# Memory's keys first, its values behind the feed-forward, queries in two pairs: a planned kernel of two transformer blocks

## The chip, the cores and the metric

The kernel runs on one core of a Trainium2 chip. The metric is the device time of one execution in microseconds (us); the median of several runs counts. What is studied here is one change to this kernel and what it does to that time.

## What is computed

Two transformer blocks, one behind the other, on 256 tokens of width 1024, batch 1, all in fp32. The first block has a modulation from a condition vector `c`, a mixer of two halves and a gated feed-forward; the second has a pooling and a top-k attention mixer, a cross-attention to 256 memory tokens, and a mixture of 32 experts (two of them per token). Cut to the part that the change touches and its neighbours:

```python
def first_block(x, c, ...):
    cond = silu(c) @ ada_w + ada_b                 # six vectors of 1024
    h = modulate(rmsnorm(x), shift1, scale1)
    x = x + gate1 * (mixer(h @ w_in) @ w_out)
    h2 = modulate(rmsnorm(x), shift2, scale2)
    g_ff, up_ff = split(h2 @ w_ffn_in)
    x = x + gate2 * ((silu(g_ff) * up_ff) @ w_ffn_out)
    return modulate(rmsnorm(x), shift_f, scale_f)  # from c, too

def memory_cross_attention(h, mem, ...):           # 4 heads of 128
    m = rmsnorm_2(mem, g_mem)
    q = rmsnorm_2(h @ w_q, q_norm)
    k = rmsnorm_2((m @ w_kv)[first half], k_norm)
    v = (m @ w_kv)[second half]
    p = softmax(q @ k.T / sqrt(128))
    return (p @ v) @ w_o

def second_block(x, mem, ...):
    x = x + concat(pool_mixer(...), dsa_attention(...)) @ w_out
    x = x + memory_cross_attention(rmsnorm_2(x), mem, ...)
    return x + hierarchical_moe(rmsnorm_2(x), ...)  # router, 32 experts
```

The memory's keys and values depend on `mem` alone, on nothing that the first block computes.

## The kernel before

**A program that is planned.** The code does not issue instructions directly. Each call on an engine (`V` VectorE, `S` ScalarE, `G` GpSimd, `PE` TensorE, `SY` SyncE, whose queue issues the DMAs) is noted by a `Recorder` (from L425) with what it reads and writes. `flush` (L709) then gives all operations of a section an order, issues them, and so decides what stands behind what on each engine; `issue` holds the one line, L763, that the profile shows for all of them. `plan` (L571) is a list scheduler: it keeps a clock for each engine, takes among the ready operations of an engine the one that can begin first and, among those that could begin now, the one of the highest priority. Priorities come from a pass backwards through the order found (`back`); `flush` repeats this in 30 rounds with random noise on the priorities and keeps the shortest plan. An operation that is ready early can thus be drawn far ahead of its place in the code, into a time in which its engine would wait.

**Memory.** 24 regions `R` (`NREG`, L246) of 128 x 2048 fp32 (1 MB) take the activations and, one after the other, the weights. These come as one long `stream` in the order of `plan()` (L211): memory's keys `mk` and values `mv` head that list, `ada` is the modulation's weights, `in_gv`, `in_v`, `in_u`, `out` are the first mixer, `fin` and `fout` the feed-forward, `in2...` and `out2` the second mixer, `wq` and `wo` the cross-attention, `gu` and `dn` the experts (96 regions). A region that is given back is filled by the next load in SP's order. 8 banks `B` of PSUM take the products.

**Products.** A weight that is used as fp32 is loaded in pieces of 1024 columns; `piece` splits each into a rounded part (ScalarE copies it to fp32r) and the rest (VectorE subtracts), and a product is then three products of 256 columns (`mm`). The halves live in smaller pools cut from regions (`rec.host`): P0, P1, P2, P3 for stages of the program (`splits`, with the numbers of `SPLITS`), and M for memory's `mk` and `mv` alone. `dense4` makes four 128-row outputs with 96 products; `moving` makes token-major outputs with 48 products of 512 columns. In the profile such operands are all called R. An fp32 product (not fp32r) leaves two records in the trace.

**The places that the change touches.** `memory()` (L1547 to 1575) makes memory's keys `km` and values `vm`: it splits `mt` (the memory, token columns), sums its squares, multiplies by `mk` (`dense4`), normalizes the keys (`k_norm_mem`), and multiplies by `mv` (`moving`). It is called at L1664, behind the second mixer's `in2v`. `mt` is loaded by a call at L1535, where `ahead` also names `mk`. Cross-attention stands at L1680 to 1742: norm `rx_` by `norm_col`, queries `wq` (`dense4`), their norm `rmq`, then for four units (head pair i, token half t) scores, maximum, exponential (`lm`), the reciprocal, transposes (`pm`), and the product with `vm`; then `wo`. `warm` (L1170, called at L1374) issues four fp32 products of `ones` by a sum, ahead of the feed-forward's norm. `xt` (x, token columns) is the first load behind the constants (L842).

Of the kernel before, what the change touches and what calls it, by code (L numbers as in the profile page):

```python
# [11 lines left out]
ALU = mybir.AluOpType  # L12
# [82 lines left out]
def layout(v):  # L95
# [51 lines left out]
    for name, arg in PLAN:  # L147
# [37 lines left out]
        elif name == "wq":  # L185
            full(rowk(wq))
# [30 lines left out]
def plan():  # L217
# [12 lines left out]
    p += [("out2", 0), ("out2", 1), ("wq", 0), ("wo", 0)]  # L230
# [10 lines left out]
def size(name, arg):  # L241
    return {("in2", 3): 1024, ("fout", 5): 2048, ("misc", 0): 3072}.get(
        (name, arg), 4096)


NREG = 24  # L246
SPLITS = (5, 6, 5, 2)
# [176 lines left out]

class Recorder:  # L425
# [3 lines left out]
    def __init__(self, nc, pools):  # L429
# [4 lines left out]
        self.total = 0.0  # L434
# [118 lines left out]
    def plan(self, prio):  # L553
# [49 lines left out]
        while len(order) < n:  # L603
# [33 lines left out]
            c = op.cost  # L637
            if op.eng == "vector" and now["gpsimd"] > t:
                c += min(c, now["gpsimd"] - t)
# [16 lines left out]
            done[op.pos] = True  # L656
            order.append((op, t, t + c))
# [53 lines left out]
    def flush(self):  # L711
# [8 lines left out]
        best, rng = None, np.random.default_rng(SEED)  # L720
        for i in range(ROUNDS):
            p = self.plan(prio)
            if best is None or p[0] < best[0]:
                best = p
                rank = [0.0] * len(ops)
                for op, s, e in p[1]:
                    rank[op.pos] = e
                base = -np.array(self.back(rank, p[4]))
                prio = list(base)
            else:  # L730
                prio = list(base + NOISE * rng.standard_normal(len(ops)))
        self.total, order, place, self.slots, _ = best
        for op, op.start, op.end in order:
# [7 lines left out]
        self.ops, self.chain = [], None  # L741

# [26 lines left out]
ROUNDS = 30  # L769
SEED = 2  # L770
NOISE = 0.5
# [9 lines left out]
def _build(tc, a, out, ctx):  # L781
# [7 lines left out]
    def region(i):  # L789
# [4 lines left out]
                        "s": tiles(20, "s", 16), "B": tiles(8, "B", 512, psum)})  # L794
# [47 lines left out]
    SY.dma_start(out=xt, in_=a["xt"])  # L842
    stage = [None]
# [20 lines left out]
    G.memset(ones, 1.0)  # L864
    inv_d = fixed(1, "inv_d")
# [26 lines left out]
    def piece(name):  # L892
# [5 lines left out]
        b = buf("M" if name in ("mk", "mv") else stage[0], 2, 1024, dt=F32R)  # L898
# [37 lines left out]
    def dense4(name, act_, pieces=range(4), ps=None):  # L936
# [4 lines left out]
        for i in pieces:  # L941
            w = piece(name)
            for kk in range(2):
                k = 2 * i + kk
                for n in range(4):
                    c = slice(512 * kk + 128 * n, 512 * kk + 128 * n + 128)
                    mm(ps[n], at(w, slice(None), c), at(act_, slice(None), k),
                       k == 0 and n % 2 == 0, k == KT - 1)
        return ps
# [88 lines left out]
    def norm_col(accs, inv):  # L1038
# [6 lines left out]
        r = small(2)  # L1045
# [124 lines left out]
    def warm(after, n):  # L1170

        ps = bank()[:, 0:T]
        for i in range(n):
            PE.matmul(out=ps, lhsT=ones, rhs=after, start=True, stop=True)

# [9 lines left out]

    sums = Sums()
# [187 lines left out]
    warm(sq2.acc[0], 4)  # L1374
# [34 lines left out]

# [137 lines left out]
    def memory():  # L1547
        for i in range(3):
            rec.host("M", Reg(), 2048)
# [447 lines left out]
```

## Time and profile before

| | |
|---|---|
| median of 3 runs | 761.04 us (759.38 to 765.29) |
| profiled execution | 763.06 us, its span 761.2 us |
| TensorE busy | 711.6 us, 93% |
| VectorE, ScalarE busy | 416.7 us (55%), 312.6 us (41%) |
| loaded | 210.48 MB, 278 GB/s over the span |

How to read it: the page divides the span into 40 slices of 19 us and gives the busy tenths of each engine in each. The chain that ended last is followed back from the last instruction, at each step to what released it. The windows give for a stretch of the span each engine's busy time with its number of records (PE, PEld, DVE, ACT, POOL in this order), then the granted TensorE clock as a share of 2.4 GHz, the DMA engines' mean share and GB/s. PE is TensorE's products, PEld its weight loads, DVE VectorE, ACT ScalarE, SP the engine that issues the loads. Because all operations are issued from one line, L763, the operands' names and shapes tell which is which: `inv_d`, `inv_h`, `ones` are constants, `cst` the table with the identity, `xt`, `mt` and `stream` the arrays in HBM. A busy PE is not a PE at its peak: the ends of products are modelled from the records around them.

### The profile page before, as it was taken

To read this page: it belongs to the slowest core of one execution; us is meant where nothing else is said; L and a number is where in the kernel's file an instruction comes from. 1 tells how busy PE (TensorE), PEld (TensorE's weight loads), DVE (VectorE), ACT (ScalarE), POOL (GpSimd) and SP (SyncE) were. 2 spreads that over 40 slices of the span, in tenths; PEclk is the share of its full clock that TensorE was granted. 3 is DMA by queue.
4 is the path that set the end of the run, shared out by engine and by line. 5 is a ranking of instruction groups with operands and counts; after the bars stand their busy time and mean duration, and the time that the engine had idled before them with its cause. 6 is when DMAs were issued, how large, how long until landed. Compare 5 with 4: busy or idle time off the path is not lost.

```text
span 761.2 us, 13000 instructions
## 1 busy us (share of the span) xinstructions
PE 711.6 (93%) x5290; PEld 555.6 (73%) x5290; DVE 416.7 (55%) x872; ACT 312.6 (41%) x597; POOL 6.9 (1%) x18
## 2 busy tenths in 40 slices
PE   4799999999999999999999999999899999987794
PEld 1487756889999999999999779898854455432231
DVE  3579847786556583797868988465612121100002
ACT  3366467233544352386845439365512111110010
POOL 0020000000000000000000000000000000000000
PEclk9999998979999999999999999999899999998898
DMA  8993689988465765743114214798879999999993
GB/s 362 420 418 139 246 311 412 370 338 314 167 215 188 262 228 174 277 139 126 65 65 127 95 56 176 237 384 303 350 292 420 422 419 421 421 421 420 421 415 127
DMA packets 31168, 212.42 MB, mean 279 GB/s; under 512 B 3584, under 2 KB 3968, under 8 KB 6272
## 3 DMA queue, kind: packets, MB, share of 16 engines
q1 hardware_dynamic: 31104, 211.55, 71.1%
q8 instruction: 43, 0.70, 0.4%
q14 instruction: 21, 0.17, 0.1%
HBM read 210.48 MB, written 1.05 MB: 278 GB/s over the span
## 4 chain that ended last, share of the span: by engine, by line
PE 76%; DMA 16%; DVE 5%; ACT 1%; issue 1%; SPq 0%; ACTq 0%; DVEq 0%
PE B L763 76%; DMA R<-stream 15%; DVE R L763 4%; DMA R<-xt 1%; DVE s L763 1%; DVE U L763 1%; ACT R L763 0%; ACT L763 0%; SPq L763 0%; ACT U L763 0%; ACT ex L763 0%; DVE cond L763 0%; DVE g L763 0%; DVE ng L763 0%; ACT s L763 0%
## 5 line engine op out<-in xcount | busy, mean ns | idle before, releaser
L763 PE MATMUL B<-R,R 128*128 128x256 f32 (+4 forms) x4376 | 592.7, 376 | 27.9 <-DVE R L763 12.8
L763 PEld LDWEIGHTS B<-R,R 128*128 128x128 f32 (+2 forms) x4376 | 436.5, 171 | 114.6 <-issue 48.7
L763 ACT ACTIVATE R<-R 128x1024 fp32r<-128x1024 f32 (+3 forms) x268 | 187.0, 737 | 168.0 <-PE B L763 120.1
L763 DVE TENSOR_TENSOR R<-R,R 128x1024 fp32r<-128x1024 f32 (+3 forms) x214 | 191.5, 930 | 62.6 <-ACT R L763 55.5
L763 DVE TENSOR_TENSOR R<-B,R 128x256 f32<-128x256 f32 (+3 forms) x78 | 33.0, 440 | 89.2 <-ACT R L763 57.2
L763 ACT ACTIVATE R<-B 128x256 f32<-128x256 f32 (+4 forms) x82 | 27.9, 370 | 80.3 <-PE B L763 80.2
L763 ACT ACTIVATE R<-B,cv 128x128 f32<-128x128 f32 (+2 forms) x64 | 25.9, 423 | 80.5 <-PE B L763 79.9
L763 PEld LDWEIGHTS B<-U,R 128*128 128x128 f32 x256 | 34.9, 196 | 28.7 <-issue 22.1
L763 PE MATMUL B<-R 128*128 128x256 f32 (+4 forms) x200 | 48.9, 378 | 1.2 <-ACT R L763 1.2
L763 DVE TENSOR_SCALAR R<-B,cv 128x128 f32<-128x128 f32 x32 | 11.1, 350 | 67.3 <-PE B L763 65.2
L763 PEld LDWEIGHTS B<-R 128*128 128x128 f32 (+1 forms) x200 | 30.9, 192 | 17.9 <-issue 12.6
L763 PE MATMUL B<-U,R 128*128 128x128 f32 x256 | 41.9, 294 | 1.8 <-DVE s L763 1.0
L763 ACT COPY R<-B 128x256 f32<-128x256 f32 (+3 forms) x35 | 13.7, 408 | 69.6 <-PE B L763 69.4
L763 DVE COPY R<-B 128x256 f32<-128x256 f32 (+2 forms) x33 | 14.8, 462 | 38.6 <-PE B L763 38.4
L763 DVE SCALAR_TENSOR_TENSOR U<-R,ca,U 128x512 f32<-128x512 f32 x42 | 31.4, 749 | 0.7
L763 DVE SCALAR_TENSOR_TENSOR R<-R,cv,R 128x256 f32<-128x256 f32 (+1 forms) x54 | 25.0, 481 | 1.8 <-ACT R L763 1.2
L763 ACT ACT_TABLE_LOAD x17 | 21.8, 1283 | 9.9 <-PE B L763 6.3
L763 PE MATMUL B<-cst,R 128*128 128x128 f32 (+3 forms) x130 | 21.8, 271 | 3.2 <-DVE R L763 3.2
L763 PEld LDWEIGHTS B<-cst,R 128*128 128x128 f32 (+1 forms) x130 | 17.6, 170 | 8.6 <-DVE R L763 5.7
L763 DVE TENSOR_TENSOR R<-R 128x256 f32<-128x256 f32 x47 | 18.2, 420 | 2.4 <-ACT R L763 1.8
L763 PE MATMUL B<-R,cst 128*128 128x256 f32 (+1 forms) x52 | 16.0, 400 | 0.1
L763 ACT ACTIVATE R<-R,cv 128x256 fp32r<-128x256 f32 (+1 forms) x28 | 12.8, 496 | 2.2 <-DVE R L763 2.1
(116 smaller groups left out, 266.0 us busy)
## 6 DMA issues: line engine op xcount, KB each, us to landing
R<-stream SPq DMA_DIRECT2D x192, 1024.0 KB, 10.4
R<-stream SPq DMA_DIRECT2D x10, 512.0 KB, 15.3
R<-xt SPq DMA_DIRECT2D x1, 1024.0 KB, 5.3
R<-mt SPq DMA_DIRECT2D x1, 1024.0 KB, 7.8
out_dram<-R SPq DMA_DIRECT2D x4, 256.0 KB, 2.1
cst<-cst SPq DMA_DIRECT2D x1, 533.0 KB, 19.6
R<-bands SPq DMA_DIRECT2D x1, 320.0 KB, 3.2
R<-cosin SPq DMA_DIRECT2D x1, 256.0 KB, 5.4
```

Of the source, the lines that this page charges most:

```text
L763: getattr(getattr(self.nc, op.eng), name)(*[real(v) for v in args], **{k: real(v) for k, v in kw.items()})
```

## The change

1. `memory()` stands at the start of the program, ahead of everything but the constants, without the values; `mt` (in two halves) and `mk` are loaded ahead of `xt`. `mk`'s and `mv`'s pieces take the stage's pool, and pool M is gone.
2. The values are a function of their own, `memory_values()`, called behind the feed-forward's last accumulation, ahead of the first block's final norm.
3. `wq` is loaded as two halves of 2048 columns, and cross-attention runs over two pairs of heads: `dense2` (48 products), norm, scores, softmax, product with `vm`, one pair behind the other.
4. 26 regions instead of 24 (`dynamic_dma_scratch_size=1024` at the build gives room); SPLITS (5, 6, 3, 2) instead of (5, 6, 5, 2), pool P3 made at the feed-forward's end already, with 2 of 5 pieces of stage P2 going to it; 18 small tiles instead of 20.
5. `warm` is gone. Where the planner sees TensorE wait longer than FILL_MIN, it puts `filler` products (`ones` by `ones`, 128 columns) into a free bank ahead of the waiting product.
6. Priorities: instead of 30 rounds with noise and the shortest plan, a list of 19 steps (`PATH`), each a pass backwards plus a `nudge`: seeded shifts of whole stretches of the program, by engine.

```diff
-            full(rowk(wq))
+            full(rowk(wq[:, 256 * arg:256 * arg + 256]))
...
-NREG = 24
-SPLITS = (5, 6, 5, 2)
+NREG = 26
+SPLITS = (5, 6, 3, 2)
...
+            if op.eng == "tensor":
+                k = min((f, i) for i, f in enumerate(slots["B"] + [1e9]) if f is not None)
+                lo = max(now["tensor"], k[0])
+                room = t - lo
+                m = int(max(FILL * room, room - FILL_END) / FILLER) if room > FILL_MIN else 0
...
-        best, rng = None, np.random.default_rng(SEED)
-        for i in range(ROUNDS):
-            p = self.plan(prio)
...
+        best = self.plan(prio)
+        for seed in PATH if self.first else (0,):
...
+            best = self.plan(list(nudge(at, seed) - np.array(self.back(rank, best[4]))))
...
+    def filler(self, m, k):
+        ones = self.ones.ap()
+        for i in range(m):
+            self.nc.tensor.matmul(out=self.pools["B"][k][:, 0:128], lhsT=ones, rhs=ones, start=True,
+                                  stop=True)
...
+FILLER, FILL, FILL_MIN, FILL_END = 0.224, 0.4, 0.7, 1.2
+PATH = (0, 4, 0, 31, 36, 0, 63, 0, 88, 120, 121, 144, 195, 343, 433, 447, 465, 779, 910)
...
-    SY.dma_start(out=xt, in_=a["xt"])
...
-        b = buf("M" if name in ("mk", "mv") else stage[0], 2, 1024, dt=F32R)
+        pool = stage[0]
+        if pool == "P2":
+            turn[0] += 1
+            pool = "P3" if turn[0] % 5 in (2, 4) else "P2"
+        b = buf(pool, 2, 1024, dt=F32R)
...
+    for k in (0, 4):
+        SY.dma_start(out=mt[:, k:k + 4], in_=a["mt"][:, k:k + 4])
+        if k == 0:
+            ahead("mk", 0, 2)
+    SY.dma_start(out=xt, in_=a["xt"])
+    rmem_ = fixed(2, "rmem", constant=False)
+    mem = memory()
...
-    warm(sq2.acc[0], 4)
...
+    splits("P3", SPLITS[3])
     splits("P2", SPLITS[2])
+    memory_values()
...
-    memory()
     attended(sums)
...
-    splits("P3", SPLITS[3])
+    stage[0] = "P3"
...
-    ps = dense4("wq", h)
...
+    for i in range(2):
+        ps = dense2("wq", h)
+        pr = bank()
```

What the planner makes of it is seen in the order of the instructions. The first place is the head of SP's queue, the loads in the order in which they are issued; the names are a region with its buffer's number, and the array in HBM. Before:

```order
L763 DMA cv<-cv 128x296
L763 DMA cst<-cst 128x164
L763 DMA R_0_144<-xt 128x2048
L763 DMA R_0_147<-stream 128x2048
L763 DMA R_0_155<-stream 128x2048
L763 DMA R_0_170<-stream 128x2048
L763 DMA R_0_180<-stream 128x2048
```

and of the change:

```order
L797 DMA cv<-cv 128x296
L797 DMA cst<-cst 128x164
L797 DMA R_0_143<-mt 128x1024
L797 DMA R_0_145<-stream 128x1024 x2
L797 DMA R_0_152<-stream 128x1024 x2
L797 DMA R_0_143<-mt 128x1024
L797 DMA R_0_219<-xt 128x2048
L797 DMA R_0_235<-stream 128x2048
L797 DMA R_0_264<-stream 128x2048
```

Ahead of `xt` there now stand `mt` in two halves and four loads of half a region each, the two regions of `mk`; the first `ada` region (`R_0_235`) follows `xt`.

The second place is TensorE at the end of the feed-forward. Before, where `R_7_3168` and `R_7_3213` are the split memory, rounded part and rest, and `R_2_3299` and `R_6_3300` regions with pieces of `mk`:

```order
L763 MATMUL B_89<-R_7_3213,R_6_3300 128x256
L763 MATMUL B_89<-R_7_3168,R_6_3300 128x256
L763 MATMUL B_87<-R_7_3168,R_2_3299 128x256
L763 MATMUL B_87<-R_7_3213,R_2_3299 128x256
L763 MATMUL B_88<-inv_d,R_0_157 128x1 x4
L763 MATMUL B_87<-R_7_3168,R_2_3299 128x256 x2
L763 MATMUL B_87<-R_7_3213,R_2_3299 128x256
L763 MATMUL B_87<-R_7_3168,R_2_3299 128x256
L763 MATMUL B_87<-R_7_3168,R_6_3300 128x256
L763 MATMUL B_87<-R_7_3213,R_6_3300 128x256
```

and of the change, where the first row is the last of the feed-forward's accumulation `R_0_154` and `R_0_158` are the split memory and `R_2_3632` holds a piece of `mv`:

```order
L797 MATMUL B_84<-R_4_1991,R_4_1360 128x256 x6
L797 MATMUL B_82<-ones,U_62 128x1 x4
L797 MATMUL B_87<-R_2_3632,R_0_154 128x512
L797 MATMUL B_83<-R_2_3632,R_0_154 128x512
L774 MATMUL B_85<-ones 128x128
L797 MATMUL B_87<-R_2_3632,R_0_154 128x512
L797 MATMUL B_87<-R_2_3632,R_0_158 128x512
L797 MATMUL B_85<-inv_d,R_0_216 128x1 x4
L797 MATMUL B_87<-R_2_3632,R_0_154 128x512
L797 MATMUL B_83<-R_2_3632,R_0_154 128x512
```

The one-column sums of the final norm (`inv_d`) now stand between 512-column products of `mv`, where before they stood between 256-column products of `mk`; a filler (`ones` by nothing else, L774) is among them.

The third place is TensorE in cross-attention, behind the products of `wq`. Before, with transposes (`cst`) of the softmax, and the products of `mv` as the 512-column rows:

```order
L763 MATMUL B_89<-R_2_3299,R_7_3168 128x512 x2
L763 MATMUL B_90<-R_6_3300,R_7_3168 128x512
L763 MATMUL B_90<-R_6_3300,R_7_3213 128x512
L763 MATMUL B_86<-cst,R_9_4984 128x128 x2
L763 MATMUL B_89<-R_2_3299,R_7_3213 128x512
L763 MATMUL B_89<-R_6_3300,R_7_3168 128x512
L763 MATMUL B_90<-R_6_3300,R_7_3168 128x512 x2
L763 MATMUL B_84<-cst,R_9_4984 128x128 x2
L763 MATMUL B_89<-R_6_3300,R_7_3168 128x512
L763 MATMUL B_90<-R_6_3300,R_7_3213 128x512
L763 MATMUL B_89<-R_6_3300,R_7_3213 128x512
```

and of the change, with the last product of `wq` at the top (`inv_h` makes the column sums of the queries' norm, and the rows with `R_0_400`, which is `km`, are the scores):

```order
L797 MATMUL B_81<-R_3_4884,R_2_3515 128x256
L797 MATMUL B_86<-inv_h,R_0_216 128x1 x4
L797 MATMUL B_87<-R_0_400,R_4_3911 128x256 x2
L797 MATMUL B_85<-inv_h,R_0_216 128x1 x4
L797 MATMUL B_88<-R_0_400,R_4_3911 128x256 x2
L797 MATMUL B_82<-R_0_400,R_4_3911 128x256 x2
L797 MATMUL B_83<-R_0_400,R_4_3911 128x256 x2
L774 MATMUL B_86<-ones 128x128 x5
L797 MATMUL B_84<-cst,R_6_5061 128x128 x2
L797 MATMUL B_86<-cst,R_6_5061 128x128 x2
```

Between the scores and the transposes there now stand five fillers, and no product of `mv` or `wq`: the last `wq` product of the second pair is ahead of the first pair's sums.

## Rows read from the trace of the kernel before

**Rows 1.** The page: the chain that ended last, shares of the span by engine.

```profile
PE 76%; DMA 16%; DVE 5%; ACT 1%; issue 1%; SPq 0%; ACTq 0%; DVEq 0%
```

**Rows 2.** The page: busy tenths in 40 slices, TensorE and DMA.

```profile
PE   4799999999999999999999999999899999987794
...
DMA  8993689988465765743114214798879999999993
```

**Rows 3.** The chain in order of time: start us, us, what.

```profile
27.50 13.32 PE B L763 x82
...
40.85 0.18 DVE cond L763
...
43.82 101.40 PE B L763 x840
...
157.49 250.86 PE B L763 x2052
...
430.16 117.32 PE B L763 x805
...
726.60 16.29 DMA R<-stream
```

**Rows 4.** Timeline of SP's issues up to 562 us: start us, us, operation, count.

```profile
485.75 58.88 SPq L763 DMA_DIRECT2D R<-stream  x21
...
555.93 5.76 SPq L763 DMA_DIRECT2D R<-stream  x5
```

**Rows 5.** Windows: stretch, its us, busy of five engines, clock, DMA share, GB/s.

```profile
43.40:46.80 3.40, 2.98 (x14) 2.98 (x15) 3.40 (x7) 0.91 (x1) 3.40 (x1) 0.51 1.02 424
...
152.60:162.80 10.20, 8.96 (x40) 8.19 (x39) 8.77 (x24) 3.01 (x7) 0.00 (x0) 0.50 1.02 430
...
385.00:410.00 25.00, 25.00 (x193) 22.01 (x192) 16.13 (x41) 12.00 (x30) 0.00 (x0) 1.00 0.18 53
410.00:430.00 20.00, 20.00 (x133) 18.03 (x131) 20.00 (x68) 13.28 (x24) 0.00 (x0) 1.00 0.29 102
430.00:440.00 10.00, 9.95 (x34) 6.17 (x34) 9.37 (x23) 2.09 (x3) 0.00 (x0) 0.83 0.32 104
495.50:540.50 45.00, 45.00 (x319) 42.22 (x318) 27.43 (x63) 25.68 (x60) 0.00 (x0) 1.00 0.90 351
540.50:556.00 15.50, 13.39 (x87) 11.51 (x89) 9.45 (x52) 8.15 (x17) 0.00 (x0) 0.67 0.60 237
...
557.00:743.00 186.00, 167.79 (x1158) 74.87 (x1158) 26.90 (x67) 23.99 (x59) 0.00 (x0) 0.97 1.01 418
```

**Rows 6.** Timeline of TensorE: start us, us, operation, count [idle before, releaser].

```profile
9.62 1.94 PE L763 MATMUL B<-R,R 128*32 128x512 f32 x8 [9.62 <-DVE R L763]
...
109.26 1.07 PE L763 MATMUL B<-R,R 128*32 128x512 f32 x8
...
326.81 25.44 PE L763 MATMUL B<-R,R 128*128 128x256 f32 x210
...
357.96 0.95 PE L763 MATMUL B<-inv_d,R 128*128 128x1 f32 x8
...
514.44 6.82 PE L763 MATMUL B<-R,R 128*128 128x512 f32 x29
...
548.58 0.64 PE L763 MATMUL B<-asum,cst 128*128 128x32 f32 x2 [1.11 <-DVE asum L763]
...
551.92 2.48 PE L763 MATMUL B<-U,R 128*128 128x128 f32 x10 [1.00 <-DVE s L763]
...
556.65 1.38 PE L763 MATMUL B<-U,R 128*128 128x128 f32 x10
...
559.82 0.49 PE L763 MATMUL B<-U,R 128*128 128x128 f32 x2
```

**Rows 7.** Timeline of ScalarE in the softmax of the cross-attention.

```profile
516.77 1.28 ACT L763 ACT_TABLE_LOAD   x1 [2.57 <-DVE s L763]
518.07 0.56 ACT L763 ACTIVATE R<-B,s,s 128x256 f32<-128x256 f32 x1
```

More of the change, by code (lines that the diff above doesn't have):

```diff
@@ L602, in plan @@
                 offer(op)
-        while len(order) < n:
+        issued = 0
+        while issued < n:
             best = None
@@ L948, in dense4, with dense2 @@
                        k == 0 and n % 2 == 0, k == KT - 1)
+        return ps
+    def dense2(name, act_):
+        b = bank()
+        ps = [b[:, T * i:T * i + T] for i in range(2)]
+        for i in range(2):
+            w = piece(name)
+            for kk in range(4):
+                k = 4 * i + kk
+                for n in range(2):
+                    c = slice(256 * kk + 128 * n, 256 * kk + 128 * n + 128)
+                    mm(ps[n], at(w, slice(None), c), at(act_, slice(None), k),
+                       k == 0 and n == 0, k == KT - 1)
         return ps
@@ L1184, in stacked, with memory, k_norm_mem, memory_values @@
         return w.rearrange("p (b m) c -> p b m c", b=4)
+    def memory():
+        hm = pair()
+        for k in range(KT):
+            split(hm, k, mt[:, k], scale=col("mn", k))
+        sums = Sums()
+        for k in range(KT):
+            sums.add(mt[:, k])
+        rmem = norm_col(sums.acc, inv_d, rmem_)
+        rmem2 = square(rmem)
+        def k_norm_mem(j, ps):
+            q = ta()
+            S.activation(out=q, in_=ps, func=AF.Square)
+            S.activation(out=km[:, j], in_=ps, func=AF.Copy, scale=col("xk_norm"))
+            p2 = bank()
+            for t in range(2):
+                PE.matmul(out=p2[:, t:t + 1], lhsT=q[:, 128 * t:128 * t + 128], rhs=inv_h, start=True,
+                          stop=True)
+            rk = small(2, 1)
+            rstd_by(rk, p2[:, 0:2].unsqueeze(2), rmem, rmem2)
+            V.tensor_tensor(out=km[:, j], in0=km[:, j], in1=norm_bc(rk[:, :, 0]), op=ALU.mult)
+        for j, ps in enumerate(dense4("mk", hm)):
+            k_norm_mem(j, ps)
+        return hm, rmem
+    def memory_values():
+        hm, rmem = mem
+        ps = moving("mv", hm)
+        for t in range(2):
+            S.activation(out=vm[:, t], in_=ps[t], func=AF.Copy, scale=rmem[:, t:t + 1])
+    for k in (0, 4):
[5 more added lines that the diff above has]
+    mem = memory()
     sums = Sums()
@@ new lines, in _build @@
+            q = ta()
+            S.activation(out=q, in_=ps[jj], func=AF.Square)
+            for t in range(2):
+                PE.matmul(out=pr[:, 2 * t + jj:2 * t + jj + 1], lhsT=q[:, 128 * t:128 * t + 128],
+                          rhs=inv_h, start=True, stop=True)
+        rmq = small(2, 2)
+        rstd_by(rmq, pr[:, 0:4].rearrange("p (t j) -> p t j", t=2), rx_, rx2)
+        V.tensor_scalar(out=rmq, in0=rmq, scalar1=128.0 ** -0.5, scalar2=None, op0=ALU.mult)
+        sume = small(2, 2)
```

170 lines of the change are left out of this document (71 added, 99 removed).

## The prediction

> **What bounds the kernel now.** First the chain of work that ended last, by engine [rows 1]: TensorE holds 76% of it, DMA 16%, VectorE 5%. The page's slices [rows 2] say which comes when: PE reads 9 from the third slice to the 35th, but for one 8, while the DMA row falls to between 1 and 4 in slices 18 to 25 and stands at 7 to 9 from there to slice 39. The chain in order of time [rows 3] gives the borders. But for its gaps at norms TensorE carries it: up to 40.82, from 43.82 to 145.22, 157.49 to 408.35 and 430.16 to 547.48; 408.35 to 430.16 is VectorE's selection. The last piece of `stream` lands at 726.60 + 16.29 = 742.89; 18.3 us of tail follow (span 761.2).
>
> The expert part is bound by transfers alone. Of 96 expert regions SP issues 21 while dense regions come back, over 58.88 us [rows 4]; then there is no free region, and the next goes at 555.93, when the first expert gives one back. From there 75 regions are moved in 742.89 - 555.93 = 186.96 us, 2.49 each, at DMA share 1.01 and 418 GB/s [rows 5]: full. So
>
> end = first expert release + 2.49 x (96 - regions filled by then) + 18.3.
>
> What shortens TensorE's way to 555.93 counts in full, and so does each region more. The profiled execution, 763.06, lies 2.0 above the median 761.04; I work out a difference on the trace and take it off the median.
>
> **Prices.** Back to back a 256-column product costs 25.44/210 = 0.121 us, a 512-column one 6.82/29 = 0.235 [rows 6]. At the lower clock 14 products fill 2.98 us, 0.213 each [rows 5]. A filler is an fp32 product of 128 columns, two records: ten such records take 1.38, two take 0.49, so a record 0.111 and a filler 0.22; at the lower clock ten take 2.48, a filler 0.43 to 0.50 [rows 6].
>
> **Start.** SP now issues 3 MB ahead of `xt` (two halves of `mt`, two regions of `mk`). At 2.49 us a region that makes `xt` and every region behind it 7.5 later. TensorE gets 96 products of `mk` (11.6 at full clock, some 20.5 at half) and 39 fillers. Before, it first works at 9.62 and then in short pieces until 27.50; that idle time takes them. What sets the dense run is not x but the last `ada` region for the condition vector, whose second half is read at 40.85, with the run at 43.82 [rows 3]. That region is now the 16th of the queue and lands at 16 x 2.49 = 39.8; behind it stand a group of eight records 1.07 [rows 6], a copy, eight condition records (about 1.5 in all) and 43.82 - 40.85 = 2.97: 45.3 to 45.8. **+2**; bounds -1.5 (the transfers hidden, the engine warm) and +7.5 (nothing hidden).
>
> **Norm ahead of the feed-forward.** `warm`'s four fp32 256-column products go, nine fillers come. From 152.6 to 162.8 the granted clock was 0.50 and 40 records took 8.96 [rows 5]. A clock that stays up saves up to 2.6 (half of 157.49 to 162.8); fillers that don't hold it cost up to 2.4. I take **-1.5**, nearer to the saving, because the order puts the nine in three of the gap's waits (2, 3 and 4), where `warm` stood in one.
>
> **Feed-forward's end to the end of `out2`,** 354.8 to 495.5. In it TensorE is the path but for the selection. What leaves: by the order 91 of 96 `mk` products stand behind the last `fout` one, 91 x 0.121 = 11.0; `norm_col` (eight one-column records, 0.95 [rows 6]), the 16 such records of `k_norm`, 1.9, and half its broadcasts, 0.9; and 13 of the 48 `mv` products, 3.1. What comes: all 48 `mv` products at the feed-forward's end, 11.3, where they cover the final norm that `mk` covered, and some fillers, 0.7. Work: 17.8 - 12 = 5.8 less. Beside it VectorE loses pieces of `mk` and `mv` next to the selection, where it is the bound: busy 20.00 of 20 from 410 on, 9.37 of 10 from 430 on [rows 5]. In those 10 us PE did 34 records at 0.83, in the 20 ahead of them 133; at that rate 34 take 5.1, so 4.9 are lost. I take 3 of them back: **-8.5**. Bounds -13 (all of it back, filling perfect) and -2 (what left was free filling of waits, and only VectorE's pieces count).
>
> **Cross-attention,** 495.5 to 540.5: PE 45.00 of 45 busy, 319 records [rows 5]. 36 `mv` products stand in it (29 in one row [rows 6]): 8.5 leave, and the other broadcasts, 0.9. They covered the softmax: the order shows them between the transposes. Its cover is now to be the second half of `wq`, but by the order all 96 `wq` products stand ahead of the first `inv_h` sums, so only five and one fillers (1.3) stand in the wait, and two more earlier. The wait behind them is square root, table load 1.28, exponentials of 0.56 [rows 7], reciprocals, transposes. Before, `wq`'s end and `wo`'s start were 16.1 us apart, of which 8.5 were `mv` and about 7.6 the softmax's own records; I put 2 of new wait and 1.8 of fillers against the 9.4: **-5.5**. Bounds -8 (the wait as short as its fillers) and -1 (the 16.1 us are latency, and `mv` was free in them).
>
> Two pairs could also cost table loads, square root and exponential being in different tables. A load takes 1.28 and the next ACTIVATE starts 1.30 after it [rows 7]; alternating pairs would add two, 2.6. ACT's order has both square roots ahead of the first exponential, with one load, so I add nothing. The Trainium skill (ScalarE: Activation LUTs, section What ACT_TABLE_LOAD costs) puts a switch at about 2.66 us, load and drain together, by which alternating would cost 5.3; no drain of that size stands behind the load in the row.
>
> **Router.** Seven fillers (1.5 at full clock, 3.3 at the lower) ahead of `asum` products that waited 1.11 for VectorE [rows 6], at a mean clock of 0.67 [rows 5]. They overrun the wait a little and may raise the clock: **0**; bounds -1.5 and +3.
>
> **Two regions more.** 23 expert regions instead of 21 ready at the first release: 2 x 2.49 = **-5.0**, if the queues can fill them. From 495.5 to 555.93 they moved 45 x 351 + 15.4 x 237 GB/s = 19.4 MB; with 2.1 more it is 21.5, and the shortened stretch of 55 us at 418 holds 23.0. Bound 0.
>
> Fillers in the expert part lie in waits for transfers: PE is busy 167.79 of 186 [rows 5]. 0. The tail stays.
>
> **Sum.** 2 - 1.5 - 8.5 - 5.5 + 0 - 5.0 = -18.5: 761.04 - 18.5 = **742.5**. On the trace: first release 555.93 - 13.5 = 542.4, last landing 542.4 + 73 x 2.49 = 724.2.
>
> **Rivals.**
> (a) Memory's products were only filling. The stretches read 45.00 of 45 because the planner puts whatever is ready into waits; without them VectorE's and ScalarE's chains show at their old length. Feed-forward to `out2` then gives -1, cross-attention 0: -5.5 in all, 755.5. For it: VectorE at 20.00 of 20. Against it: from 385 to 410 VectorE is busy 16.13 of 25 and PE full [rows 5]; there products are the path.
> (b) The regions are not ready at the first release, because it comes 13.5 earlier while dense regions come back late: -13.5, 747.5. For it: only 1.5 MB of room in the sum above. Against it: the DMA share of 0.60 ahead of the release [rows 5], with nothing free to fill.
> (c) Slower: the start runs in sequence at the lower clock. 39 fillers at 0.43 (16.8), 96 `mk` products at 0.213 (20.5), eight `ada` groups at 1.94, as at 9.62 (15.5), the 59 `in_gv` products ahead of the run (12.6) and some 7 us of steps on other engines: dense run at 72.7, +29 in place of +2, 769.5. It decides from about 72 on. For it: the row at 9.62 is at that slow rate, against 1.07 later [rows 6]. Against it: from 27.50 on 82 products take 13.32 [rows 3], 0.162 each, so the clock had come up by then with less work than now.
>
> **How the numbers follow.** (a) 0.12, (b) 0.10, (c) 0.06, the forecast the rest, 0.72, with a range of its own of 734 to 750: the start's +7.5 or the cross-attention's -1 reach up, the feed-forward's -13 and the start's -1.5 down. A measurement here tells about 1% from no change: below 753.4, above 768.7. Faster is the forecast and (b), 0.82; same (a), 0.12; slower (c), 0.06. The range 733 to 754 takes in (b) and leaves out (a)'s centre and (c), 0.18.
>
> **What would show it.** Dense run at 45 to 46; products behind the first norm at full clock before 160; about 132 us instead of 140.7 from the feed-forward's end to `out2`'s end; some 10 us from `wq`'s end to `wo`; first release near 542, 73 regions behind it at 2.49, last landing near 724. It is wrong if the dense run begins after 50, if PE waits over 4 us in the softmax, if `out2` ends as late behind the feed-forward as before, or if fewer than 23 expert regions are full at the release.

## The result, and the profile of the changed kernel

The changed kernel took 751.23 us (median of 4) where the kernel before took 762.94 beside it: a ratio of 0.9872 over all executions (0.985 by the two medians), 95% interval 0.9835 to 0.991. Run once more, beside other executions of before, it took 751.19 against 763.7, 0.9846 (0.9812 to 0.988). It is faster by 1.3 to 1.5%. Forecast were 742.5 and 2.4%: the time lies in the range, the gain is little more than half of the forecast. Executions more than 1.5% above the fastest of their kernel (one of 761.16 and two of over 1700 below) are in no median or ratio here.

The page of the changed kernel, profiled at 751.32 (span 749.6); first its slices, then the shares of its chain by engine:

```profile
PE   9999999999999999999999999999999999987894
...
PEclk9999999999999999999999999999999999999898
DMA  8997389996458668655621325973799999999981
...
PE 86%; DMA 7%; DVE 3%; ACT 1%; SPq 1%; issue 1%; ACTq 0%
```

Against [rows 1] and [rows 2], TensorE now holds 86% of the chain and transfers only 7 where they held 16, although the DMA row still stands at 9 from slice 30 to 38. That is the first sign of what went wrong: the transfers are as dense as before, but they no longer set the end. In the chain in order of time (start us, us, what) the last wait for a transfer ends at 696.34, 53 us ahead of the end; in [rows 3] it ended at 742.89:

```profile
49.30 96.31 PE B L797 x831
...
157.03 194.72 PE B L797 x1624
...
539.71 98.69 PE B L797 x751
...
676.45 19.89 DMA R<-stream
...
698.99 10.79 PE B L797 x40
709.78 0.64 PE B L774 x4
710.42 1.84 PE B L797 x8
712.26 0.64 PE B L774 x4
...
731.10 1.01 PE B L797 x4
```

L774 are fillers: from 709.78 on they stand in the chain itself.

The next table cuts both programs at the same places. A border is the start or end of a stage's products in the trace, found by counting TensorE's records along the order of the program; the first release is the SP issue of the first expert load that had to wait for a region, and the last landing the end of the last weight packet among the DMA records (4.6 us behind the 742.89 of [rows 3], which is the last one that the chain waits for). Each kernel was profiled twice; the last column is the mean of the two differences.

| stretch, us | before | again | changed | again | forecast | measured |
|---|---|---|---|---|---|---|
| start to the end of `out` | 147.6 | 148.4 | 149.1 | 149.9 | +2 | +1.5 |
| to the last `fout` product | 207.2 | 207.0 | 202.7 | 202.7 | -1.5 | -4.4 |
| to the end of `out2` | 140.8 | 140.7 | 138.5 | 138.5 | -8.5 | -2.2 |
| to the end of `wo` | 45.0 | 45.0 | 40.0 | 40.0 | -5.5 | -5.0 |
| to the first expert release | 15.4 | 15.4 | 12.4 | 12.4 | 0 | -3.0 |
| to the last landing | 191.6 | 191.4 | 187.4 | 187.3 | -5.0 | -4.2 |
| to the end | 13.7 | 14.9 | 19.7 | 19.7 | 0 | +5.3 |
| sum | 761.2 | 762.8 | 749.6 | 750.4 | -18.5 | -12.0 |

The first release came at 542.56, as forecast (542.4), but by other steps; the stream behind it was shortened nearly as forecast; the end then lost 5. Two stages of the sum, the one up to `out2` and the tail, are wrong by 6 and 5. Up to the release the errors cancel (6.3 too little gained up to `out2`, against 2.9 and 3.0 more than forecast up to `fout` and at the router), which was luck; of the 6.5 us that are missing in the end, 5.3 are the tail's.

SP's timeline behind the feed-forward (start us, us, operation, count) has the first release where [rows 4] had 555.93:

```profile
542.56 6.07 SPq L797 DMA_DIRECT2D R<-stream  x6
```

### The profile page after: what moved, and what is told of

Read it like the earlier page. It is cut to its first block, busy times and chain, and to the rows that moved or that the text cites. A ratio compares the mean times of both kernels' runs of the same rounds, so it can differ in the third digit from the quotient of the medians.

```text
span 749.6 us, 13378 instructions
## 1 busy us (share of the span) xinstructions
PE 718.4 (96%) x5466; PEld 569.5 (76%) x5466; DVE 418.1 (56%) x876; ACT 311.3 (42%) x597; POOL 3.7 (0%) x18
## 4 chain that ended last, share of the span: by engine, by line
PE 86%; DMA 7%; DVE 3%; ACT 1%; SPq 1%; issue 1%; ACTq 0%
PE B L797 85%; DMA R<-stream 7%; DVE R L797 2%; ACT R L797 1%; SPq L797 1%; PE B L774 1%; DVE s L797 0%; DVE U L797 0%; DVE gi L797 0%; DVE g L797 0%; DVE lgt L797 0%; DVE j L797 0%; DVE cond L797 0%; DVE i L797 0%; DVE ei L797 0%
## 5 line engine op out<-in xcount | busy, mean ns | idle before, releaser
L797 PE MATMUL B<-R,R 128*128 128x256 f32 (+4 forms) x4376 | 580.5, 366 | 12.3 <-DMA R<-stream 7.9
L797 ACT ACTIVATE R<-R 128x1024 fp32r<-128x1024 f32 (+4 forms) x268 | 187.9, 738 | 160.5 <-PE B L797 122.4
L797 DVE TENSOR_TENSOR R<-B,R 128x256 f32<-128x256 f32 (+3 forms) x78 | 32.8, 440 | 72.3 <-ACT R L797 58.1
L797 PE MATMUL B<-U,R 128*128 128x128 f32 x256 | 40.2, 287 | 1.1 <-ACT R L797 0.7
L774 PEld LDWEIGHTS B<-ones 128*128 128x128 f32 x184 | 26.4, 217 | 13.9 <-issue 10.9
L774 PE MATMUL B<-ones 128*128 128x128 f32 x184 | 30.9, 313 | 1.5 <-POOL inv_h L797 1.4
```

The costliest lines, as they stand in the source:

```text
L774: self.nc.tensor.matmul(out=self.pools["B"][k][:, 0:128], lhsT=ones, rhs=ones, start=True, stop=True)
L797: getattr(getattr(self.nc, op.eng), name)(*[real(v) for v in args], **{k: real(v) for k, v in kw.items()})
```

## Experiments

### The fillers

The order of all other instructions was kept in these three; only `flush` issues fewer of the fillers that the plan has. The first leaves out the 28 behind the router:

```diff
+        runs = 0
         for x in order:
             if len(x) == 2:
-                self.filler(*x)
+                runs += 1
+                if runs <= 11:
+                    self.filler(*x)
                 continue
```

> The changed kernel with the same order of all other instructions, without the 28 fillers behind the router (experts and tail). Theory: the last transfers came 17.6 us earlier than before, but the end only 11.6, because TensorE is late in the last 35 us, and of that 4.5 us are fillers that stand in its way (the chain has 0.6% of the span on their line). Then the end comes 3 to 4.5 us earlier, about 747, and TensorE shows small gaps for transfers again from 696 on. Rival 1: the fillers only take up time in which TensorE waits anyway, and the order of the expert products makes it late: within 1 us of the changed kernel. Rival 2: the fillers hold the clock up; without them it falls to half in more of 680 to 735 and the end comes later by 2 or more.

Measured: 751.28 (median of 6), 0.9869 (0.9836 to 0.9901). In the trace the end came 15.7 us behind the last landing instead of 19.7, as the theory has it. Its profiled execution took 749.29 with a first release 1.7 later than the changed kernel's. But the medians don't show the 4 us: the time is that of rival 1.

The second leaves out all 92 (`if len(x) == 2: continue`).

> The changed kernel, same order, without any of the 92 fillers. Theory: at the start, TensorE's first mk products run at the lower clock, but the start is bound by the landing of the ada regions, so the dense run begins within 1 us of 49.3; the gap before the feed-forward (149.08 to 156.91) grows by 1 to 2 us; the router's by up to 2; the tail gains as in the run without the expert fillers. First expert release 3 us later than 542.6, the end about as in the changed kernel. Rival: the fillers at the start carry the clock, and without them the dense run begins 5 us or more later.

Measured: 751.22 (median of 6), 0.9881 (0.9839 to 0.9922). The end of `out` came at 148.9 and the feed-forward began at 156.6, against 149.1 and 156.9: the 39 fillers of the start and the nine ahead of the feed-forward moved neither. The first `in_gv` product even came 1.8 earlier. Only the seven of the router earn something, as two windows from the end of `wo` to the first release show (columns as in [rows 5]), the changed kernel's first, then the one without fillers:

```profile
530.20:542.60 12.40, 11.68 (x104) 10.54 (x107) 9.72 (x53) 7.61 (x17) 0.00 (x0) 1.00 0.71 268
```

```profile
531.60:546.90 15.30, 14.37 (x90) 12.25 (x92) 9.78 (x53) 7.81 (x17) 0.00 (x0) 0.67 0.58 223
```

With the fillers the granted clock stays at 1.00 and the stretch takes 12.4; without them it is 0.67 and 15.3, as before the change (15.4, and 0.67 in [rows 5]). 15.7 us lay between the last landing and the end. So the 3 us that fillers earn at the router, those in the experts give back. (The profiles that keep the router's seven agree on the 12.4: 12.3 or 12.4 in all five.)

The third keeps the fillers from the norm ahead of the feed-forward to the router alone (`if 3 <= runs <= 11`).

> The changed kernel in the same order, with the fillers of the start and of the experts left out and those from the norm ahead of the feed-forward to the router kept. Theory: the start is bound by transfers and needs no filler; the router's fillers hold the clock (12.4 us from the last wo product to the first release, 15.3 without); the experts' fillers cost 4 us between the last landing and the end (19.7 against 15.7). So the trace shows all of that and the time is 2 to 4 below the changed kernel's in this call. Rival: what the experts' fillers cost they give back by a clock that falls less (7.5 us at half clock between first release and last landing, 18.7 without them), and the time is the same within 1.

Measured: 750.18 (median of 5), 0.9837 (0.9803 to 0.987), beside 751.19 of the changed kernel; the spreads (746.8 to 752.3, 749.3 to 754.6) overlap, so a gain of 1 is not proved, and the theory's 2 to 4 did not come; the time is that of the rival. The trace has what the theory said of it: first release 542.49, and 15.5 from the last landing to the end. TensorE's timeline at the same place in both, the changed kernel first:

```profile
709.71 0.71 PE L774 MATMUL B<-ones 128*128 128x128 f32 x4
710.35 1.91 PE L797 MATMUL B<-R,R 128*32 128x512 f32 x8
712.19 0.71 PE L774 MATMUL B<-ones 128*128 128x128 f32 x4
712.83 1.91 PE L797 MATMUL B<-R,R 128*32 128x512 f32 x8
...
728.23 1.05 PE L797 MATMUL B<-R,R 128*32 128x512 f32 x4
729.21 0.49 PE L774 MATMUL B<-ones 128*128 128x128 f32 x2
729.63 1.05 PE L797 MATMUL B<-R,R 128*32 128x512 f32 x4
```

```profile
705.03 1.91 PE L800 MATMUL B<-R,R 128*32 128x512 f32 x8
707.45 1.91 PE L800 MATMUL B<-R,R 128*32 128x512 f32 x8 [0.51 <-DMA R<-stream]
709.94 1.91 PE L800 MATMUL B<-R,R 128*32 128x512 f32 x8 [0.58 <-DMA R<-stream]
```

Without fillers each group of eight begins when its load lands: 2.4 and 2.5 us apart, half a us of it a wait. With them a group and its four filler records fill the whole 2.48 from one group to the next (709.71 to 712.19), so TensorE does not wait here and does not catch up either. The chain says the same; in the kernel without them it is transfers up to 709.90:

```profile
648.71 19.87 DMA R<-stream
...
668.64 20.19 DMA R<-stream
...
688.90 21.00 DMA R<-stream
...
709.94 1.94 PE B L800 x8
```

So the planner put fillers where its plan saw a wait, and here they made TensorE later.

### The values at the feed-forward's end

```diff
+        products = [op for op in rec.ops[n:] if op.eng == "tensor"]
+        rec.skip, rec.kept = {id(op) for op in products[6:42]}, products
...
     def issue(self, op):
+        if id(op) in self.skip:
+            return
```

> The changed kernel in the same order, but 36 of the 48 products of mv at the feed-forward's end are left out (only the first and last of the eight groups of the sum are made, so memory's values are not computed in full). Theory: in that gap TensorE waits for the pieces of mv and for the norm's steps on ScalarE and VectorE, so what leaves is mostly filling: the 15.5 us from the last feed-forward product to the first of the second mixer shrink by 2 to 4, and the first expert release comes 2 to 4 earlier. Rival (my forecast's bookkeeping): products there are the path, 36 x 0.235 = 8.5 leave, and the release comes 7 or more earlier.

Measured: TensorE left the feed-forward at 354.81 and began the second mixer at 367.21, 12.4 later instead of 15.5. So 36 products of 0.235 gave 3.1 us, not 8.5, and nothing remained of it: `out2` ended 139.1 behind the feed-forward (138.5 in the changed kernel), the first release was at 546.29, 3.7 later than in the changed kernel, of which 3.1 were there at the feed-forward's end. The 3.1 of the gap are in the theory's 2 to 4, its earlier release is not. (Behind that, the other values send other loads to the experts, and the whole, 1007.72, says nothing of this gap.) TensorE's timeline in that gap, without the 36:

```profile
358.36 0.71 PE L801 MATMUL B<-R,R 128*128 128x512 f32 x2
360.39 0.71 PE L801 MATMUL B<-R,ones 128*128 128x128 f32 x4 [1.32 <-DVE R L801]
360.86 1.41 PE L801 MATMUL B<-R,R 128*128 128x512 f32 x5
367.21 2.71 PE L801 MATMUL B<-R,R 128*128 128x256 f32 x10 [4.95 <-ACT R L801]
```

The wait of 4.95 is ended by ScalarE: the norm's broadcast, gain and square steps on VectorE and ScalarE bound the gap at about 12 in this order, with a quarter of TensorE's products left in it (11.5 in before, with `mk`). And the ten products behind the wait took 0.27 each, so the clock had fallen; the window from 367.2 to 380 has it at 0.66, against 1.00 in the changed kernel (the first row is without the 36 products, the second the changed kernel):

```profile
367.20:380.00 12.80, 12.79 (x74) 12.69 (x75) 9.97 (x20) 9.65 (x19) 0.00 (x0) 0.66 0.36 124
```

```profile
367.20:380.00 12.80, 12.80 (x105) 12.45 (x104) 11.32 (x23) 11.24 (x24) 0.00 (x0) 1.00 0.31 98
```

So most of the value products were filling there, and what they added to the gap they gave back by the clock behind it, as far as one execution shows.

### The two regions

Before with 26 regions and the changed kernel with 24 are each an edit of one number (the first with the smaller scratch and 18 small tiles too, for the room), with a new order by the planner:

```diff
-NREG = 24
+NREG = 26
```

> The kernel before with 26 regions (and the smaller scratch, 18 small tiles, to make room), nothing else; the planner makes a new order. Theory: 23 instead of 21 expert regions are filled at the first release, the transfers end 5 us earlier than before relative to the first release, and as TensorE still waited for transfers in the last 50 us there, the end follows: about -4 to -5 us (756 to 757). Rival: TensorE's own work in the last 50 us is the bound as soon as transfers come earlier, and the two regions give 0 to -2.

> The changed kernel with 24 regions, a new order by the planner. Theory: transfers end 4 to 5 us later relative to the first release, but the end of the program stays or moves by less than 2, because in the changed kernel TensorE, not the transfers, sets the last 35 us. Rival: transfers still set the end, and it comes 4 to 5 us later (755 to 756).

Measured: 752.78 against 761.5 for before with 26, 0.9888 (0.9845 to 0.9931), more than the theory's 4 to 5 us; 763.97 for the changed kernel with 24, 1.0039 (1.0016 to 1.0062). Both expectations of the second failed: it is slower than the kernel before. With the two regions alone, before has almost the whole gain.

The list of shifts was made for one set of operations, so the changed kernel was also run with the old search and without fillers, with 26 and with 24 regions:

```diff
+        best, rng = None, np.random.default_rng(SEED)
+        for i in range(ROUNDS):
+            p = self.plan(prio)
...
-        best = self.plan(prio)
-        for seed in PATH if self.first else (0,):
...
-FILLER, FILL, FILL_MIN, FILL_END = 0.224, 0.4, 0.7, 1.2
+FILLER, FILL, FILL_MIN, FILL_END = 0.224, 0.0, 0.7, 1.2
```

> The changed kernel with its order searched as before (30 rounds with noise, the shortest plan) and no fillers; memory first, two pairs and 26 regions stay. Theory (the regions carry the change): 26 regions alone made the kernel before 7.5 us faster, the other parts together are worth some 3, so this is about like the kernel before with 26 regions, 752 to 757. Rival: the shifted priorities are what makes memory first and two pairs pay, and without them the time is 759 or more.

> The same with 24 regions: memory first, values at the feed-forward's end, two pairs, in an order searched as before. Theory: without the regions these parts gain nothing, 759 to 765, as the changed kernel with 24 regions (764.0) said; its list of shifts was then not at fault. Rival: that list was only unfit for 24 regions, and the parts themselves gain about 5: 754 to 757.

Measured: 753.67 with 26, 0.9876 (0.9842 to 0.9909), as the theory has it; 768.42 with 24, 1.0071 (1.0043 to 1.0098), slower than theory and rival said.

| kernel | ratio to before | first release | last landing | end (span) |
|---|---|---|---|---|
| before, 24 regions | 1 | 555.9 | 747.5 | 761.2 |
| before, 26 | 0.9888 | 547.1 | 733.9 | 750.9 |
| changed, 24 | 1.0039 | 549.4 | 741.6 | 761.1 |
| changed, 26 | 0.9872 | 542.6 | 729.9 | 749.6 |
| changed, old search, no fillers, 24 | 1.0071 | 555.9 | 748.8 | 767.9 |
| changed, old search, no fillers, 26 | 0.9876 | 549.5 | 736.8 | 753.8 |

In each pair the stream behind the release takes 4.8 to 5.6 us less with 26, as the sum had it. But the release itself comes 6.4 to 8.8 earlier, for which the sum had nothing. SP's timeline at the first release of before with 26 regions:

```profile
547.10 4.60 SPq L763 DMA_DIRECT2D R<-stream  x4
```

To see whether the stages ahead gain by having the regions, two were held in the kernel with the old search until the cross-attention's norm:

```diff
+    held = [view(Reg(), 0, 2) for i in range(2)]
+    for r in held:
+        G.memset(r, 0.0)
...
     rx_ = norm_col(sq4_.acc, inv_d)
+    for r in held:
+        V.tensor_tensor(out=r, in0=r, in1=rx_, op=ALU.add)
```

> As the kernel with the old search and 26 regions, but two regions are written with zeros at the start and held until the norm of the cross-attention, so that all stages ahead have 24 and the experts 26. Theory A (the stages ahead gain by the regions themselves): the first release comes as with 24 regions, 554 to 557, the stream then takes 187 (23 regions ready), and the whole is 758 to 762. Theory B (the new order, not the regions): the first release comes as with 26, 548 to 551, and the whole is 752 to 756.

Measured: 764.16, 1.0029 (1.0002 to 1.0056), with the first release at 558.04, where the 24 regions put it (555.91), not the 26 (549.49), and 23 expert regions ready:

```profile
558.04 5.58 SPq L801 DMA_DIRECT2D R<-stream  x5
```

The release is theory A's, though 2 late, and the whole is 2 above its 758 to 762. That is no proof of it. The last experiment of the next part shows how much a new order does by itself, and by the granted-clock records this execution spent 44.3 us at half clock up to the release, against 30.0 with 26 regions and 32.8 with 24; up to half of such a difference can be the clock's.

### The keys

With the old search and 26 regions, `memory()` was moved behind the feed-forward, with the values, and `xt` made the first load:

```diff
-    for k in (0, 4):
-        SY.dma_start(out=mt[:, k:k + 4], in_=a["mt"][:, k:k + 4])
-        if k == 0:
-            ahead("mk", 0, 2)
     SY.dma_start(out=xt, in_=a["xt"])
...
-    mem = memory()
...
     splits("P2", SPLITS[2])
+    SY.dma_start(out=mt, in_=a["mt"])
+    mem = memory()
     memory_values()
```

> As the kernel with the old search and 26 regions, but the memory's keys too are made at the end of the feed-forward, and x is again the first load. Theory: 3 MB ahead of x cost 6 us by the end of the first mixer (149.08 against 142.99 in the kernel before with 26 regions), and that comes back; the 96 key products then fill waits of the second mixer as before. End of the first mixer near 143, the whole 2 to 5 us faster than with the keys first. Rival: the keys' products are on the path behind the feed-forward and take 11 us there, while at the start they cost 6: 3 to 6 us slower.

Measured: 755.54, 0.991 (0.9875 to 0.9944), against 753.67 and 0.9876 with the keys first: no faster, as the theory had it, and the intervals overlap, so that the rival's 3 to 6 slower is not shown either. `out` ended at 140.3 instead of 147.5: in these two traces the keys at the start cost 7.2 us there, where my sum had +2. But from the first product of the second mixer to the attention it took 82.5 instead of 67.2. The keys' work is paid at either place.

Then the loads and `memory()` were put behind the first modulation weights (the removed lines above, ahead of `ypad`):

> As the kernel with the old search and 26 regions, but mt and mk are loaded behind x, the modulation's first weights and the first in_gv regions, and the keys' work is recorded there. Theory: the 3 MB ahead of x are what delays the first mixer (its end 147.5 with keys first, 140.3 with the keys at the feed-forward's end); behind the first weights they delay nothing that waits, and the 11.6 us of key products partly fill waits for transfers: end of the first mixer near 144, the whole 2 to 4 us faster than with the keys first. Rival: TensorE's work is the path from there on, wherever the keys stand, so the first mixer ends at 147 to 150 and the time is the same within 1.

Measured: 751.46, 0.9841 (0.981 to 0.9872). The first `in_gv` product came at 26.2 instead of 33.5, but `out` ended at 147.4, as with the keys first (147.5): the rival's outcome at that place. So it does not look as if the transfers ahead of x were what the keys cost there; that TensorE pays for their products is argued and not shown, as each order ends `out` elsewhere. The whole is as fast as the changed kernel, with the old search and without a filler; it is 2.2 below the keys first, as the theory had it, but the intervals overlap.

Last, that kernel with fillers planned between the feed-forward and the experts alone:

```diff
-                if m and k[1] < len(slots["B"]) and FILL:
+                if m and k[1] < len(slots["B"]) and self.lo <= op.pos < self.hi:
```

> The kernel with mt and mk loaded behind x (old search, 26 regions), with fillers planned only between the feed-forward and the experts. From its trace without fillers: 14.5 us from the last wo product to the first release, of which the changed kernel's fillers save 2 to 3. So 748 to 750, about 2 below the kernel without fillers and 1 to 3 below the changed kernel. Rival: another order, and the same time.

Measured: 760.18, 0.9965 (0.994 to 0.999), 9 slower. The fillers are late in the program, but the whole order is new, and `out` now ends at 152.6 instead of 147.4, long ahead of any filler. Both executions spent 3.4 us at half clock ahead of it, so a change that cannot matter there costs 5 us by the order alone. SP's timeline at the first release, 6.5 us later than the 547.58 without these fillers:

```profile
554.07 6.07 SPq L801 DMA_DIRECT2D R<-stream  x6
```

### Both kernels once more

> The changed kernel once more, as a measure of how far one profiled execution stands for all: 749 to 754, stages within 3 us of the first profile, with other stretches of half clock.

> The kernel before once more, one look: 758 to 765, stages within 3 us of the first profile.

Measured: 751.19 and 764.52. The stages of the table above repeat within 1.3 us. That flatters the first row: the kernel without the expert fillers and the one with few value products have the changed kernel's instructions up to `out`, and ended it at 151.7 and 151.5 where the changed kernel had 149.1 and 149.9. So a difference of under 3 us in a single trace can be that of one execution.

## Why the prediction was wrong in two steps

**Start: +2 forecast, +1.5 measured, by luck.** `mk`'s products did run while TensorE had waited, 47 of them by 18.63, but the dense run began at 49.30, 5.5 later than before, and not at 45.5. In the profiled execution 4 came back behind it, because before had half the granted clock from 115 to 122 and the changed kernel had not. Windows of before, the changed kernel, before with 26 regions, and the changed kernel without the expert fillers, whose instructions up to there are the changed kernel's:

```profile
115.00:122.00 7.00, 7.00 (x32) 2.65 (x28) 5.21 (x13) 3.92 (x11) 0.00 (x0) 0.51 1.01 421
```

```profile
115.00:122.00 7.00, 7.00 (x64) 3.00 (x56) 4.85 (x12) 5.90 (x12) 0.00 (x0) 1.00 1.02 424
```

```profile
115.00:122.00 7.00, 7.00 (x57) 4.39 (x57) 5.15 (x13) 5.82 (x14) 0.00 (x0) 1.00 1.01 420
```

```profile
115.00:122.00 7.00, 7.00 (x40) 2.11 (x36) 3.87 (x9) 5.12 (x11) 0.00 (x0) 0.60 1.01 423
```

The last row says that this is no property of the change. The four executions with the same instructions up to `out` spent 0, 3.4, 6.8 and 6.8 us at half clock ahead of it, and ended it at 149.1, 149.9, 151.7 and 151.5; before spent 10.2 in both of its own. Over the four, the start is some 2.5 us longer than before's. Nor do 26 regions keep the clock up: with the old search and 26 regions it stood at half from 116.6 to 123.5. With the keys moved away `out` ended 7.2 earlier, but in another order; the upper bound of 7.5 may have been the better value, though not for the reason given (transfers).

**Norm and feed-forward: -1.5 forecast, -4.4 measured.** The direction holds. Without any filler it was still 204.2 from `out` to the last `fout` product, -2.9: the greater part is not theirs. Of the rest, about 1.6, they may have a share; two more profiles with the same nine fillers, without the expert fillers and with few value products, took 203.4 and 203.3.

**Feed-forward's end to `out2`: -8.5 forecast, -2.2 measured; this step failed.** I added up products that leave and enter, as if TensorE were the bound in each piece of the stretch (and took 8.5 from a sum of 5.8 and 3, which is 8.8). It is not in the gap of the final norm: that was 11.5 us in before with `mk` in it and became 15.5 with `mv`; with a quarter of `mv`'s products it was 12.4, its last wait ended by ScalarE. The 4 us by which the gap grew are two thirds of the error. In the rest of the stretch the work that left did shorten it, by 6.2: from the second mixer's first product to `out2`'s end 129.2 in before, 123.0 in the changed kernel. The 3 us for the selection did not come either. Windows of the changed kernel, ahead of the selection's end and at it:

```profile
405.00:425.00 20.00, 20.00 (x147) 18.06 (x146) 14.29 (x35) 11.41 (x26) 0.00 (x0) 1.00 0.46 159
425.00:434.00 9.00, 9.00 (x37) 5.88 (x37) 8.75 (x34) 1.43 (x2) 0.00 (x0) 1.00 0.01 2
```

VectorE has less to do ahead of it, 14.29 of 20 us where [rows 5] had 20.00, but at the end it is as full as before, and TensorE makes 37 records in 9 us there. At the rate of the row above, 4.0 us are lost, where the prediction had 4.9: about 1 came back. Rival (a) came nearest at this stage (-1). Its reason, that a busy TensorE whose planner fills waits does not show which products are needed, holds for the gap; the 6.2 of the rest speak against it.

**Cross-attention: -5.5 forecast, -5.0 measured.** Right, with its reason: from `wq`'s end to `wo` 11.3 us instead of 18.5, by the first `wo` product (the prediction's 16.1 ended at 525.18, with other products ahead of `wo`). TensorE waited 0.97, 0.17 and 0.28 between the groups of transposes, and fillers stood in the rest. The table load that alternating pairs would have added did not come: the profile has 16 loads instead of 17.

**Router: 0 forecast, -3.0 measured.** Beyond the lower bound of -1.5: the fillers held the clock at 1.00 through the gather, too.

**Two regions: -5.0 forecast, -4.2 measured in the stream** (4.8 to 5.6 in the pairs). The term is right, and in each pair two loads less were left at the release, against rival (b). Its place among the causes was not right: of the forecast 18.5 I gave them 5, and by the pairs they are nearly all of the change's gain (0.9888 of 0.9872). Without them the moved work, the pairs, the fillers and the shifts together made the kernel 0.4% slower. With 24 regions they do bring the first release forward by 6.6 (549.4 against 555.9), and the tail takes 5.9 of it back.

**Tail: 0 forecast, +5.3 measured; this step failed.** "Fillers in the expert part lie in waits for transfers" was read from TensorE's mean idle time there, 18 of 186 us. But a mean says nothing of the single wait. In the changed kernel from 679 to 689 a group of eight takes 1.07 us of the 2.5 between two landings, and four filler records fit behind it:

```profile
678.92 1.07 PE L797 MATMUL B<-R,R 128*32 128x512 f32 x8 [0.56 <-DMA R<-stream]
679.91 0.71 PE L774 MATMUL B<-ones 128*128 128x128 f32 x4
681.42 1.07 PE L797 MATMUL B<-R,R 128*32 128x512 f32 x8 [0.79 <-DMA R<-stream]
```

From 705 on a group takes 1.91, 0.6 is left, and the four take 0.71 (the rows of the fillers' part above). The 1.91 is not the lower clock, which is granted at 1.00 from 709.7 to 714.7; so the 1.94 of the group at 9.62 [rows 6], which rival (c) took for the slow rate, need not be the clock either. Without the fillers 4.1 of the 5.3 are gone; the remaining 1 to 2 I have not traced. "The tail stays" had no reason in the sum: without any filler, the other orders have tails from 13.4 to 19.1 us.

What stays open is why the two regions bring the first release forward by 6 to 9. Holding them back took that away, and in three pairs it has the same sign; but each kernel has its own order, and a new order alone moved the release by 6.5. The clock is a part of it. Up to the first release the granted clock was at half for 34.0 us in before and 16.7 with 26 regions, 20.4 in the changed kernel with 24 and 6.8 with 26, 32.8 and 30.0 in the pair with the old search. If all of that time were TensorE's, half of each difference would come back: 8.7 of the 8.8 us in the first pair, 6.8 of 6.8 in the second, but 1.4 of 6.4 in the third. Whether the regions, the orders or the single executions (30.6 in before's second profile, 10.2 in the changed kernel's) made the clock stay up is not shown.

No version beat the changed kernel clearly. The one with fillers from norm to router alone has the lowest median, 750.18, and the shortest profiled span, 745.1 against 749.6 and 750.4, but that execution is the fastest of its five, and the medians' difference of 1 is within their spread.

## What to carry to other kernels

Where a scheduler fills waits with whatever is ready, a busy engine does not show that its work is the bound: moving work away from such a stretch pays only up to the chain of the other engines under it, so price that chain first, gap by gap. Deeper buffering of a stream can be worth more than the moved work around it, and is one number to try alone. Idle work that is meant to keep a clock up belongs only where a wait is certain: in a stretch that is nearly full it delays the work behind it. And a trace is one execution: compare a stage over several profiles of the same order before a difference of 2 or 3 us is given a cause.

## What the runs showed of the hardware

By the granted-clock records, half-clock stretches come at about the same places for the same order of instructions, but not each time and not equally long. Before spent 10.2 us at half clock up to the end of `out` in both of its profiled executions, and 10.2 and 10.2 from `wo` to the first release. The changed kernel spent 0 and 3.4 up to `out`, and two more kernels with the same instructions up to there 6.8 each, with TensorE busy 7.00 of 7 us in the row above (0.60). The fall near 115 us does not follow a wait: in eight profiles that have it, TensorE has no idle time over 0.15 us in the 30 us ahead of it. What it does there, in the kernel without the expert fillers (at half from 113.7 to 120.6), are products of few rows and columns:

```profile
111.24 0.51 PE L800 MATMUL B<-cst,U 128*128 128x2 f32 x4
111.61 0.36 PE L800 MATMUL B<-R,R 128*128 128x256 f32 x1
111.81 0.28 PE L800 MATMUL B<-cst,U 128*128 128x2 f32 x2
112.02 2.13 PE L800 MATMUL B<-R,cst 8*128 8x256 f32 x8
```

The changed kernel makes the same products there, and in one of its executions the clock did not fall.

Seven fillers (1.73 us in the trace) in a wait ahead of the router's sums kept the clock at 1.00 over the whole stretch to the first release in all five profiles that have them, and shortened it by 2.9 us, 1.7 times their own length. The 39 at the start moved nothing that the traces show.
